# In the first mixer of a two-layer model, VectorE makes every lower weight part, and the closing scans of a head move behind the next head's gate projection

## The chip, the core and the metric

The kernel runs on one core of a Trainium2 chip. The metric is the device time of one execution in microseconds. Engine names in the rows: PE is TensorE, PEld its weight loads, DVE is VectorE, ACT is ScalarE, POOL is GpSimd, SP is SyncE, which issues the loads of weights.

## What is computed

A two-layer backbone over 256 latent tokens and 256 context tokens of width 1024. Layer 0 mixes tokens with a bidirectional gated linear recurrence, layer 1 with a spatial gate, and a mixture of 64 experts follows each mixer. The change touches the first mixer alone:

```python
def rglru_mixer(hx, hc, w_in, conv_w, conv_b, ..., w_out, ctx_out):
    gate_x, ux = jnp.split(hx @ w_in, 2, axis=-1)
    ux = dwconv_centred(ux, conv_w, conv_b)
    uc = dwconv_centred(hc @ w_in[:, RNN_WIDTH:], conv_w, conv_b)
    for d in range(2):                       # both directions
        a_c, b_c = lru_coeffs(flip(uc), ...)  # a = exp(log_a), b = sqrt(1 - a*a) * i * u
        h_c = linear_scan(a_c, b_c)          # h[t] = a[t] * h[t-1] + b[t]
        a_x, b_x = lru_coeffs(flip(ux), ...)
        b_x = b_x.at[:, 0].add(a_x[:, 0] * h_c[:, -1])
        yx = yx + flip(linear_scan(a_x, b_x))
    return (jax.nn.gelu(gate_x) * yx) @ w_out
```

The recurrence is 1280 wide, in five heads of 256.

## The kernel before

Instructions are issued in the order in which the program is written, each engine works its own list from the front, and an instruction that waits holds up all behind it on its engine.

**Products in three parts.** A product in full precision is three TensorE products of rounded parts: upper weight times upper input, upper weight times lower input, lower weight times upper input (`mm3`, L311 and on; all recorded at L307). The upper weight part `wh` is a rounding copy of a piece of 128x512 on ScalarE (L563). The lower part `wl` is the piece less `wh` (L564), on the engine that `eng` returns. `splitter` hands out pieces in order and makes each up to three ahead of its use; `wh` and `wl` have four buffers, so the fifth piece waits until TensorE has read the first. A tile of weights (1 MB) is four pieces.

**The stage.** After a start, in which the inputs are normalised and the first projection runs interleaved with small products for the modulation (`first_quarter`), `plan0` sets the order of five heads h = 0 to 4. For each: A(h) projects to the two halves (i = 0, 1) of the recurrence's input, C(h) projects to the gate, B(h) makes the recurrence's coefficients; one to four filler products (F, matrix tiles of the modulation, no lower parts) stand between them. Then four output tiles O(0) to O(3) use heads 0 to 3, and Q uses head 4.

- A(h) takes one tile. After each half, `conv` runs: ScalarE scales one tap (L753), VectorE adds three (L755, `uc`), casts the result to its upper part (L758, `us`) and subtracts for the lower part (L759).
- C(h) takes one tile and ends in a Gelu on ScalarE (L858).
- B(h) takes one tile and does two column blocks jt = 0, 1. For each, ScalarE computes tanh and exp from eight products (L817 to L823), then VectorE runs a **chain** of four operations of 128x1024 on `te`, `ta`, `ti` (L825 to L828). The block is put into `held`.
- `B_end` **closes** a block: a square root on ScalarE (L833), then on VectorE a product (L836), four scans of 128x256 (L840, L843) and a sum (L845). `release` closes the oldest held block. Before the change both blocks of head h-1 are closed at the end of A(h).
- `gated(h)` multiplies a closed head with its gate (L868, VectorE) and splits it into `zh` and `zl` (L869, L870): on GpSimd for heads 0 to 3, on VectorE for head 4.
- `decay`, issued once behind A(0), makes the recurrence's decay coefficients `nz` from `lam`: an exp on ScalarE (L789) and 27 VectorE operations of 128x20 (L790 to L802).

The chooser of the engine for `wl` before the change: the fillers have no lower parts, and all tiles of A, C, O and B go to GpSimd, those of Q to VectorE.

Of the kernel before, what the change touches and what calls it, by code (L numbers as in the profile page):

```python
# [14 lines left out]
AF = mybir.ActivationFunctionType  # L15
# [286 lines left out]
def _body(nc, tc, a, pp, rp, ps, ps1, dr):  # L302
    V, S, G, PE = nc.vector, nc.scalar, nc.gpsimd, nc.tensor
    st = Stream(nc)

    def mm(out, lhsT, rhs, start, stop):
        PE.matmul(out, lhsT, rhs, start=start, stop=stop, skip_group_check=True)  # L307

    def mm3(out, wh, wl, xh, xl, start, stop):

        mm(out, wh, xh, start, False)  # L311
        mm(out, wh, xl, False, False)
        mm(out, wl, xh, False, stop)

    def bank(shape=(P, 512)):
        return ps.tile(list(shape), F32, name="b")
# [22 lines left out]
    plan0, nf = [], 0  # L339
# [9 lines left out]
    for kind, i in plan0[1:]:  # L349
# [10 lines left out]
        elif kind == "F":  # L360
            l, c, k = fillers[i]
# [92 lines left out]
    def warm(func):  # L454

        S.activation(out=warm_t, in_=onesf[:, 0:1], func=func)
# [96 lines left out]
    def splitter(tmp, tiles, eng, bufs=4):  # L553

        out = []

        def get(q, last=None):
            while len(out) < min(q + 3, last or 4 * len(tiles)):
                i, c = divmod(len(out), 4)
                t = st.tile(tiles[i])[:, 512 * c:512 * c + 512]  # L560
                hi = tmp.tile([P, 512], F32R, name="wh", bufs=bufs)
                lo = tmp.tile([P, 512], F32R, name="wl", bufs=bufs)
                S.copy(out=hi, in_=t)  # L563
                eng(i, c).tensor_tensor(out=lo, in0=t, in1=hi.bitcast(F32), op=OP.subtract)  # L564
                out.append((hi, lo))
                if c == 3:
                    st.free(tiles[i])
            return out[max(q, 0)]

        return get  # L570

    def cut(parts, c):
        return [x[:, c * P:c * P + P] for x in parts]
# [63 lines left out]
    def mixer0(rx):  # L637
      with tc.tile_pool(name="m0", bufs=1) as mp, tc.tile_pool(name="m0t", bufs=2) as tp:
# [3 lines left out]
        def h0(x, k):  # L642
            return h0t[2 * x + k // 4][:, k % 4, :]
# [31 lines left out]
        for half in range(2):  # L675
            q = [qc[k // 4] if half else qx[:, k:k + 4] for k in (0, 4)]
# [3 lines left out]
            q = q[0]  # L680
# [20 lines left out]
        sx = mp.tile([P, 8], F32, name="sx")  # L701
        sc = mp.tile([P, 8], F32, name="sc")

        def split_eng(i, c):
            kind, j = plan0[users[i]]
            return G if kind in "ACOB" else V

        users = [i for i, e in enumerate(plan0) if e[0] != "F"]

        base = 8  # L710
        wq = splitter(tp, [2] + [base + i for i in users[1:]], split_eng)

        def first_quarter(b):

# [29 lines left out]
        def A(h, q):  # L744
            uc = tp.tile([P, 2, 2, T], F32, name="uc", bufs=2)
            us = tp.tile([P, 2, 2, 512], F32R, name="us", bufs=1)
            ucs[h] = uc, us

            def conv(i, p):
                ft = 2 * h + i  # L750
                pv = p.rearrange("p (s t) -> p s t", s=2)
                o = uc[:, i]
                S.activation(out=o, in_=pv, func=AF.Identity, scale=cw[:, 2, ft:ft + 1], bias=cb[:, ft:ft + 1])  # L753
                for kk, (d0, d1, s0_, s1_) in ((0, (2, T, 0, T - 2)), (1, (1, T, 0, T - 1)), (3, (0, T - 1, 1, T))):
                    V.scalar_tensor_tensor(out=o[:, :, d0:d1], in0=pv[:, :, s0_:s1_], scalar=cw[:, kk, ft:ft + 1],  # L755
                                           in1=o[:, :, d0:d1], op0=OP.mult, op1=OP.add)
                of = o.rearrange("p s t -> p (s t)")
                V.tensor_copy(out=us[:, 0, i, :], in_=of)  # L758
                V.tensor_tensor(out=us[:, 1, i, :], in0=of, in1=us[:, 0, i, :].bitcast(F32), op=OP.subtract)  # L759

            ps_ = [bank(), bank()]
            steps = [(i, k) for k in range(8) for i in range(2)] if h == 0 else [(i, k) for i in range(2) for k in range(8)]
            for i, k in steps:
                if h == 0 and i == 0 and k:
                    yield
                wc = divmod(2 * k + i if h == 0 else 8 * i + k, 4)
                mm3(ps_[i], *cut(wq(q + wc[0], 4 if h == 0 and k < 7 else None), wc[1]), h0(0, k), h0(1, k), k == 0, k == 7)
                if k == 7:
                    wq(q + 3 + 2 * i)
                    conv(i, ps_[i])  # L770
            release()
            release()

        held, done = deque(), []
        first_quarter(0)
        assert st.reserve("a_in") == 2
        a0 = A(0, 0)
# [26 lines left out]
        def B(h, q):  # L804
            warm(AF.Exp)
            uc, us = ucs.pop(h)
            y = ys[h] = tp.tile([P, 2, T], F32, name="hf", bufs=4)

            for jt in range(2):
                ft = 2 * h + jt  # L810
                ta, te, ti = (tp.tile([P, 2, 512], F32, name=n, bufs=2) for n in ("T", "Tt", "I"))
                for g in range(2):
                    for d in range(2):
                        p = bank()
                        for k in range(2):
                            mm3(p, *cut(wq(q + 2 * jt + g), 2 * d + k), us[:, 0, k, :], us[:, 1, k, :], k == 0, k == 1)
                        S.activation(out=(ta, ti)[g][:, d, :], in_=p, func=AF.Tanh, scale=0.5, bias=(rb_, ib_)[g][:, d, ft:ft + 1])  # L817
                if jt:
                    wq(q + 5)
                for d in range(2):  # L820
                    n1, n2 = nz[:, d, ft:ft + 1], nz2[:, d, ft:ft + 1]
                    S.activation(out=te[:, d, :], in_=ta[:, d, :], func=AF.Tanh, scale=n1, bias=n1)
                    S.activation(out=ta[:, d, :], in_=ta[:, d, :], func=AF.Exp, scale=n2, bias=n2)  # L823
                uv = uc[:, jt].rearrange("p s t -> p (s t)").unsqueeze(1).to_broadcast([P, 2, 512])
                V.scalar_tensor_tensor(out=te, in0=ta, scalar=1.0, in1=te, op0=OP.add, op1=OP.mult)  # L825
                V.tensor_scalar(out=ta, in0=te, scalar1=-1.0, scalar2=1.0, op0=OP.mult, op1=OP.add)
                V.scalar_tensor_tensor(out=te, in0=te, scalar=2.0, in1=te, op0=OP.subtract, op1=OP.mult)
                V.scalar_tensor_tensor(out=ti, in0=ti, scalar=1.0, in1=uv, op0=OP.add, op1=OP.mult)  # L828
                held.append((h, jt, y, ta, te, ti))

        def B_end(h, jt, y, ta, te, ti):

            S.activation(out=te, in_=te, func=AF.Sqrt, scale=-0.25)  # L833
            V.memset(te[:, 0, T:T + 1], 0.5)
            V.memset(te[:, 1, 2 * T - 1:2 * T], 0.5)
            V.tensor_tensor(out=ti, in0=ti, in1=te, op=OP.mult)  # L836
            for d in range(2):
                r_, s_, i_ = ta[:, d, :], te[:, d, :], ti[:, d, :]
                rv = (lambda z: z[:, ::-1]) if d else (lambda z: z)
                V.tensor_tensor_scan(rv(s_[:, T:]), rv(r_[:, T:]), rv(i_[:, T:]), 0.0, OP.mult, OP.add)  # L840
                last = T if d else 2 * T - 1
                dst = s_[:, :T] if d else y[:, jt, :]
                V.tensor_tensor_scan(rv(dst), rv(r_[:, :T]), rv(i_[:, :T]), s_[:, last:last + 1], OP.mult, OP.add)  # L843
                if d:
                    V.tensor_tensor(out=y[:, jt, :], in0=y[:, jt, :], in1=dst, op=OP.add)  # L845
            if jt:
                if h < 4:
                    done.append(h)
                else:
                    gated(h)  # L850

        def Cg(i, q):
            p = bank()
            for j in range(2):
                for k in range(8):
                    mm3(p[:, j * T:(j + 1) * T], *cut(wq(q + 2 * j + k // 4), k % 4), h0(0, k)[:, :T], h0(1, k)[:, :T], k == 0, k == 7)
            gs[i] = tp.tile([P, 2, T], F32, name="hf", bufs=4)
            S.activation(out=gs[i].rearrange("p f t -> p (f t)"), in_=p, func=AF.Gelu_apprx_tanh)  # L858

        ob = {}  # L860
        def release():
            if held:
                B_end(*held.popleft())

        def gated(h):
# [29 lines left out]
        for i, (kind, j) in enumerate(plan0):  # L895
            if kind == "F":
                l, c, k = fillers[j]
# [14 lines left out]
            n = st.reserve({"A": "a_in", "C": "a_in", "B": "gate", "O": "a_out", "Q": "a_out"}[kind])  # L912
# [688 lines left out]
    with tc.tile_pool(name="rx", bufs=1) as rx:  # L1601
        tail = mixer0(rx)
        tail = moe(0, tail)
        tail = mixer1(tail)
        moe(1, tail)
# [16 lines left out]
```

## Time and profile before

| | us |
|---|---|
| median of three runs (lowest to highest) | 1508.54 (1504.59 to 1512.67) |
| the profiled execution | 1504.02 |
| its span, first to last instruction | 1502.2 |
| PE busy in the span | 1410.3 (94%) |
| DVE busy | 766.5 (51%) |
| ACT busy | 518.9 (35%) |
| POOL busy | 433.7 (29%) |
| the first mixer, to its last update of x | 0 to 257.05 |

The shares are means over stages with different limits: the first mixer is the one stage in which VectorE and GpSimd are busy most of the time. What the change is worth is to be read in the first 257 us.

### The profile page before, as it was taken

To read this page: it belongs to the slowest core of one execution; us is meant where nothing else is said; L and a number is where in the kernel's file an instruction comes from. 1 tells how busy PE (TensorE), PEld (TensorE's weight loads), DVE (VectorE), ACT (ScalarE), POOL (GpSimd) and SP (SyncE) were. 2 spreads that over 40 slices of the span, in tenths; PEclk is the share of its full clock that TensorE was granted. 3 is DMA by queue.
4 is the path that set the end of the run, shared out by engine and by line. 5 is a ranking of instruction groups with operands and counts; after the bars stand their busy time and mean duration, and the time that the engine had idled before them with its cause. 6 is when DMAs were issued, how large, how long until landed. Compare 5 with 4: busy or idle time off the path is not lost.

```text
span 1502.2 us, 27457 instructions
## 1 busy us (share of the span) xinstructions
PE 1410.3 (94%) x10752; PEld 983.3 (65%) x10752; DVE 766.5 (51%) x1388; ACT 518.9 (35%) x901; POOL 433.7 (29%) x454
## 2 busy tenths in 40 slices
PE   5999898789999999999999999789999999999998
PEld 4767677546567565565747899666656666566665
DVE  6899997623343434334346686532425333333434
ACT  4767673321222222222225544422212212212232
POOL 1666665412222113221101361322212212211210
PEclk9999999899999999999999999899999999999998
DMA  9776575589998999999999854469998999999994
GB/s 376 280 278 228 224 308 224 231 318 377 381 418 358 421 420 406 421 394 420 420 418 380 320 169 153 140 231 391 362 396 358 421 421 409 406 402 422 420 420 168
DMA packets 77446, 514.88 MB, mean 343 GB/s; under 512 B 9856, under 2 KB 10240, under 8 KB 17024
## 3 DMA queue, kind: packets, MB, share of 16 engines
q1 hardware_dynamic: 74720, 508.91, 83.8%
q10 hardware_dynamic: 2592, 4.16, 0.8%
q8 instruction: 86, 1.41, 0.4%
q14 instruction: 48, 0.39, 0.1%
HBM read 511.99 MB, written 1.05 MB: 342 GB/s over the span
## 4 chain that ended last, share of the span: by engine, by line
PE 59%; issue 13%; POOL 3%; DVE 2%; DMA 2%; ACT 1%; ACTq 0%; POOLq 0%; SPq 0%; DVEq 0%
PE b L307 49%; PE s L307 10%; DMA wr<-in_m_gu 2%; POOL S L1399 1%; POOL wl L564 1%; PE b L1475 1%; DMA wr<-in_m_dn 1%; DVE wl L564 1%; DVE h L948 0%; ACT wh L563 0%; PE b L1587 0%; DVE v L1004 0%; DVE xT L1115 0%; DVE v L1067 0%; DVE u L956 0%
## 5 line engine op out<-in xcount | busy, mean ns | idle before, releaser
L564 POOL TENSOR_TENSOR wl<-wr,wh 128x512 fp32r<-128x512 f32 x134 | 208.2, 1570 | 537.0 <-ACT wh L563 534.8
L307 PE MATMUL b<-wr,xg 128*32 128x512 f32 (+2 forms) x1496 | 301.1, 602 | 8.2 <-DMA wr<-in_m_gu 6.3
L563 ACT CAST wh<-wr 128x512 fp32r<-128x512 f32 x256 | 152.4, 618 | 200.8 <-PE b L307 93.6
L307 PE MATMUL b<-wx,xg 128*32 128x512 f32 (+1 forms) x712 | 196.1, 599 | 0.0
L307 PEld LDWEIGHTS b<-wr,xg 128*32 128x32 f32 (+2 forms) x1496 | 83.3, 119 | 130.6 <-issue 107.2
L307 PE MATMUL s<-hh,wh 128*128 128x256 f32 x512 | 153.7, 300 | 6.4 <-ACT wh L563 6.4
L564 POOL TENSOR_TENSOR wl<-wx,wh 128x512 fp32r<-128x512 f32 x48 | 71.4, 1505 | 302.5 <-ACT wh L563 263.5
L1115 DVE SCALAR_TENSOR_TENSOR xT<-b,mod,xT 128x256 f32<-128x256 f32 x304 | 130.0, 478 | 49.1 <-PE b L307 43.2
L564 DVE TENSOR_TENSOR wl<-wr,wh 128x512 fp32r<-128x512 f32 x122 | 100.2, 838 | 104.3 <-ACT wh L563 104.2
L1491 DVE SCALAR_TENSOR_TENSOR Y<-b,gt,Y 128x512 fp32r<-128x512 f32 x88 | 66.1, 751 | 169.4 <-ACT Y L1490 169.4
L307 PE MATMUL s<-hh,wl 128*128 128x256 f32 x512 | 146.9, 287 | 3.4 <-POOL wl L564 3.4
L307 PE MATMUL b<-wr,ht 128*32 128x512 f32 (+2 forms) x752 | 148.1, 599 | 1.5 <-ACT ht L1477 1.4
L307 PE MATMUL s<-hl,wh 128*128 128x256 f32 x512 | 145.9, 285 | 0.0
L1468 DVE TENSOR_TENSOR h<-h,b 128x256 f32<-128x256 f32 x44 | 18.5, 420 | 205.3 <-ACT h L1467 205.3
L307 PEld LDWEIGHTS s<-hh,wh 128*128 128x128 f32 x512 | 99.4, 194 | 36.0 <-issue 28.3
L1490 ACT ACTIVATE Y<-b,gt 128x512 fp32r<-128x512 f32 x88 | 60.5, 687 | 136.0 <-PE b L307 136.0
L1467 ACT ACTIVATE h<-b 128x256 f32<-128x256 f32 x44 | 16.9, 383 | 256.4 <-PE b L307 256.4
L307 PEld LDWEIGHTS s<-hh,wl 128*128 128x128 f32 x512 | 99.4, 194 | 4.5 <-POOL wl L564 4.2
L307 PEld LDWEIGHTS s<-hl,wh 128*128 128x128 f32 x512 | 99.6, 194 | 0.4
L307 PE MATMUL b<-wx,ht 128*32 128x512 f32 (+2 forms) x352 | 99.1, 603 | 0.5 <-ACT ht L1477 0.5
L563 ACT CAST wh<-wx 128x512 fp32r<-128x512 f32 x112 | 66.5, 618 | 93.9 <-PE b L307 48.3
L1399 POOL TENSOR_SCALAR S<-cst,agq 128x32 fp32r<-128x32 f32 (+3 forms) x208 | 82.6, 421 | 49.4 <-PE b L307 49.3
(283 smaller groups left out, 2817.5 us busy)
## 6 DMA issues: line engine op xcount, KB each, us to landing
wr<-in_m_gu SPq DMA_DIRECT2D x173, 1024.0 KB, 11.6
wx<-in_m_gu SPq DMA_DIRECT2D x83, 1024.0 KB, 11.9
wr<-in_m_dn SPq DMA_DIRECT2D x82, 1024.0 KB, 10.8
wx<-in_m_dn SPq DMA_DIRECT2D x40, 1024.0 KB, 9.9
wr<-in_ada_w SPq DMA_DIRECT2D x31, 1024.0 KB, 7.8
wr<-in_a_in SPq DMA_DIRECT2D x10, 1024.0 KB, 8.7
wr<-in_ada SPq DMA_DIRECT2D x8, 1024.0 KB, 12.2
wr<-in_b_v SPq DMA_DIRECT2D x7, 1024.0 KB, 16.3
```

Of the source, the lines that this page charges most:

```text
L307: PE.matmul(out, lhsT, rhs, start=start, stop=stop, skip_group_check=True)
L563: S.copy(out=hi, in_=t)
L564: eng(i, c).tensor_tensor(out=lo, in0=t, in1=hi.bitcast(F32), op=OP.subtract)
L1115: V.scalar_tensor_tensor(out=xT[:, d, :], in0=y, scalar=mod[:, l, 5, d:d + 1], in1=xT[:, d, :], op0=OP.mult, op1=OP.add)
L1399: (G if b else V).tensor_scalar(out=s[:, tt, i * P + o:i * P + o + wd], in0=C["iota1"][:, j:j + wd], scalar1=agq[:, tt, q:q + 1], scalar2= ...
L1467: S.activation(out=h, in_=p[:, :256], func=AF.Silu)
L1468: V.tensor_tensor(out=h, in0=h, in1=p[:, 256:], op=OP.mult)
L1475: PE.transpose(p[:, k * P:(k + 1) * P], h[:, k * P:(k + 1) * P], ident)
L1490: S.activation(out=hi, in_=p, func=AF.Copy, scale=gts[g])
L1491: V.scalar_tensor_tensor(out=y[:, 1, 512 * c:512 * c + 512], in0=p, scalar=gts[g], in1=hi.bitcast(F32), op0=OP.mult, op1=OP.subtract)
```

## The change

1. All lower parts of the mixer's weights are made on VectorE (76 pieces move from GpSimd; the four of Q were there).
2. In `conv`, the cast to the upper part moves from VectorE to ScalarE (L758).
3. Pieces are split ahead: `ready(n)` makes all pieces up to the n-th, ahead of the convolutions, of the chains of B and of the closings.
4. A head's two closings move from the end of A(h) to the end of C(h), one ahead of one more split piece and one behind it. Their square roots (`roots`) stay at the end of A(h).

```diff
-        def split_eng(i, c):
-            kind, j = plan0[users[i]]
-            return G if kind in "ACOB" else V
-
         users = [i for i, e in enumerate(plan0) if e[0] != "F"]
 
         base = 8
-        wq = splitter(tp, [2] + [base + i for i in users[1:]], split_eng)
+        wq = splitter(tp, [2] + [base + i for i in users[1:]], lambda i, c: V)
+
+        def ready(n):
+
+            wq(n - 3)
...
                 of = o.rearrange("p s t -> p (s t)")
-                V.tensor_copy(out=us[:, 0, i, :], in_=of)
+                S.copy(out=us[:, 0, i, :], in_=of)
                 V.tensor_tensor(out=us[:, 1, i, :], in0=of, in1=us[:, 0, i, :].bitcast(F32), op=OP.subtract)
...
                 if k == 7:
-                    wq(q + 3 + 2 * i)
+                    ready(q + 6 + 2 * i)
                     conv(i, ps_[i])
-            release()
-            release()
+            roots()
...
-                if jt:
-                    wq(q + 5)
+
+                ready(q + 6 + 2 * jt)
                 for d in range(2):
...
+        def roots():
+
+            while len(rooted) < len(held):
+                te = held[len(rooted)][4]
+                S.activation(out=te, in_=te, func=AF.Sqrt, scale=-0.25)
+                rooted.append(te)
+
         def B_end(h, jt, y, ta, te, ti):
-
-            S.activation(out=te, in_=te, func=AF.Sqrt, scale=-0.25)
...
+            ready(q + 8)
             gs[i] = tp.tile([P, 2, T], F32, name="hf", bufs=4)
             S.activation(out=gs[i].rearrange("p f t -> p (f t)"), in_=p, func=AF.Gelu_apprx_tanh)
+            release()
+            ready(q + 9)
+            release()
 
         ob = {}
+
         def release():
             if held:
+                if not rooted:
+                    roots()
+                rooted.popleft()
                 B_end(*held.popleft())
```

TensorE's and SyncE's lists are the same before and after, but for which buffer a load goes to. Three places of the other lists matter.

**VectorE around the decay coefficients**, behind A(0): first before, then after. `s_...` and `lam` are the small 128x20 operands, `nz` the coefficients, `Tt` and `T` the operands of B(0)'s first chain, `wr_298` the weight tile of B(0) and `wr_382` that of A(1).

```order
L799 TENSOR_TENSOR s_185<-s_185,s_183 128x20
L800 TENSOR_SCALAR s_184<-lam 128x20
L801 SCALAR_TENSOR_TENSOR nz<-s_185,s_184 128x20
L802 TENSOR_SCALAR nz_182<-nz 128x20
L825 SCALAR_TENSOR_TENSOR Tt<-T,Tt 128x1024
```

```order
L798 TENSOR_TENSOR s_185<-s_185,s_183 128x20
L799 TENSOR_SCALAR s_184<-lam 128x20
L800 SCALAR_TENSOR_TENSOR nz<-s_185,s_184 128x20
L801 TENSOR_SCALAR nz_182<-nz 128x20
L564 TENSOR_TENSOR wl<-wr_298,wh 128x512 x4
L564 TENSOR_TENSOR wl<-wr_382,wh 128x512 x2
L824 SCALAR_TENSOR_TENSOR Tt<-T,Tt 128x1024
```

The four lower parts that B(0)'s products read, before on GpSimd's list, now stand on VectorE's list behind the last coefficient.

**ScalarE around A(2)'s second half and C(2)**, first before, then after. The weight tiles are C(2)'s (`wr_869` before, `wr_853` after) and B(2)'s (`wr_959`, `wr_963`); `hf<-b` is the Gelu, `Tt<-Tt` the square roots of head 1.

```order
L563 CAST wh<-wr_869 128x512 x2
L753 ACTIVATE uc<-b,cb,cw 128x512
L833 ACT_TABLE_LOAD
L833 ACTIVATE Tt<-Tt 128x1024 x2
L563 CAST wh<-wr_959 128x512 x2
L858 ACT_TABLE_LOAD
L858 ACTIVATE hf<-b 128x512
L563 CAST wh<-wr_959 128x512 x2
```

```order
L563 CAST wh<-wr_853 128x512 x2
L753 ACTIVATE uc<-b,cb,cw 128x512
L758 CAST us<-uc 128x512
L834 ACT_TABLE_LOAD
L834 ACTIVATE Tt<-Tt 128x1024 x2
L563 CAST wh<-wr_963 128x512 x4
L863 ACT_TABLE_LOAD
L863 ACTIVATE hf<-b 128x512
```

The cast of `uc`, which reads what VectorE adds, now stands ahead of the table load, the square roots and the upper parts of B(2).

**VectorE from A(2)'s convolutions to the closings of head 1**, first before, then after; `wr_853` is C(2)'s tile, `wr_963` B(2)'s, and the MEMSET opens a closing.

```order
L755 SCALAR_TENSOR_TENSOR uc<-b,cw,uc 128x2x254
L755 SCALAR_TENSOR_TENSOR uc<-b,cw,uc 128x2x255 x2
L758 CAST us<-uc 128x512
L759 TENSOR_TENSOR us<-uc,us 128x512
L834 MEMSET Tt 128x1
```

```order
L564 TENSOR_TENSOR wl<-wr_853,wh 128x512 x2
L755 SCALAR_TENSOR_TENSOR uc<-b,cw,uc 128x2x254
L755 SCALAR_TENSOR_TENSOR uc<-b,cw,uc 128x2x255 x2
L759 TENSOR_TENSOR us<-uc,us 128x512
L564 TENSOR_TENSOR wl<-wr_963,wh 128x512 x4
L838 MEMSET Tt 128x1
```

The pieces show the second half of A(2). Between the convolution and the first closing VectorE now has the four lower parts of B(2), whose upper parts ScalarE makes behind its square roots.

## Rows read from the trace of the kernel before

**Rows 1.** Windows: us, busy us of PE, PEld, DVE, ACT, POOL; PEclk, DMA share, GB/s.

```profile
0.00:61.53 61.53, 45.56 (x436) 35.72 (x440) 44.46 (x117) 34.36 (x56) 17.14 (x16) 1.00 0.96 381
61.53:95.92 34.39, 33.40 (x191) 24.48 (x184) 33.44 (x35) 25.53 (x38) 22.43 (x12) 1.00 0.64 254
95.92:134.21 38.29, 34.90 (x181) 25.63 (x180) 35.19 (x38) 25.57 (x38) 25.72 (x15) 0.91 0.68 252
...
170.78:208.37 37.59, 32.84 (x166) 25.22 (x163) 35.63 (x37) 24.30 (x36) 25.15 (x14) 0.91 0.56 224
208.37:257.05 48.68, 43.23 (x322) 37.28 (x320) 42.13 (x45) 23.12 (x39) 36.63 (x23) 0.96 0.65 259
```

**Rows 2.** Waits, 20 to 257 us: total us, times, longest.

```profile
PE b L307 <- POOL wl L564: 13.2, 9, 4.7
```

**Rows 3.** Timeline, PE, 97.5 to 102: start, us, work, idle before.

```profile
101.54 0.79 PE L307 MATMUL b<-wx,wl 128*128 128x512 f32 x1 [3.39 <-POOL wl L564]
```

**Rows 4.** Windows: the stretch of lowered clock behind that wait.

```profile
100.38:107.20 6.82, 5.66 (x13) 4.46 (x14) 5.99 (x4) 3.46 (x5) 6.82 (x4) 0.50 0.08 32
```

**Rows 5.** Timeline, DVE, head 2's chain to head 2's closing.

```profile
134.21 1.22 DVE L825 SCALAR_TENSOR_TENSOR Tt<-T,Tt 128x1024 f32<-128x1024 f32 x1 [0.74 <-ACT T L823]
135.47 1.66 DVE L826 TENSOR_SCALAR T<-Tt 128x1024 f32<-128x1024 f32 x1
137.16 2.18 DVE L827 SCALAR_TENSOR_TENSOR Tt<-Tt 128x1024 f32<-128x1024 f32 x1
...
152.24 0.43 DVE L758 CAST us<-uc 128x512 fp32r<-128x512 f32 x1
152.70 0.69 DVE L759 TENSOR_TENSOR us<-uc,us 128x512 fp32r<-128x512 f32 x1
153.31 2.31 DVE L755 SCALAR_TENSOR_TENSOR uc<-b,cw,uc 128x508 f32<-128x508 f32 x3
...
164.35 0.06 DVE L835 MEMSET Tt<- 128x1 f32 x1
...
168.94 0.22 DVE L919 CAST identb<-cst 128x128 bf16<-128x128 f32 x1
```

**Rows 6.** Timeline, POOL, the same head.

```profile
136.54 15.84 POOL L564 TENSOR_TENSOR wl<-wr,wh 128x512 fp32r<-128x512 f32 x8
```

**Rows 7.** Timeline, DVE, Q's lower parts, with GpSimd at rest.

```profile
245.79 2.49 DVE L564 TENSOR_TENSOR wl<-wx,wh 128x512 fp32r<-128x512 f32 x4
```

**Rows 8.** Timeline, ACT, behind A(3)'s second half.

```profile
150.50 1.28 ACT L833 ACT_TABLE_LOAD   x1
151.79 2.01 ACT L833 ACTIVATE Tt<-Tt 128x1024 f32<-128x1024 f32 x2
153.71 1.12 ACT L563 CAST wh<-wr 128x512 fp32r<-128x512 f32 x2
```

**Rows 9.** Timeline, DVE, the coefficients and the first chain.

```profile
50.85 0.17 DVE L790 TENSOR_SCALAR s<-s 128x20 f32<-128x20 f32 x1
...
54.49 1.26 DVE L797 TENSOR_TENSOR s<-s,s 128x20 f32<-128x20 f32 x1
...
58.22 0.18 DVE L802 TENSOR_SCALAR nz<-nz 128x20 f32<-128x20 f32 x1
61.53 1.23 DVE L825 SCALAR_TENSOR_TENSOR Tt<-T,Tt 128x1024 f32<-128x1024 f32 x1 [3.14 <-ACT T L823]
```

**Rows 10.** Timeline, PE, B(0): first and last of 32 merged rows, 48 products.

```profile
49.78 0.63 PE L307 MATMUL b<-us,wh 128*128 128x512 f32 x2
...
60.91 0.39 PE L307 MATMUL b<-us,wl 128*128 128x512 f32 x1
```

**Rows 11.** Timeline, PE, one step of Q (12 products, 8 router products).

```profile
252.15 0.36 PE L307 MATMUL b<-zh,wh 128*128 128x256 f32 x1
...
253.66 1.00 PE L307 MATMUL s<-rws,xT 128*128 128x64 f32 x8
254.47 0.37 PE L307 MATMUL b<-zh,wh 128*128 128x256 f32 x1
```

More of the change, by code (lines that the diff above doesn't have):

```diff
@@ L768, in A @@
                 if k == 7:
-                    wq(q + 3 + 2 * i)
+                    ready(q + 6 + 2 * i)
                     conv(i, ps_[i])
-            release()
-            release()
-        held, done = deque(), []
+            roots()
+        held, rooted, done = deque(), deque(), []
         first_quarter(0)
```

## The prediction

> **What bounds the kernel now.** I cut the start of the span into windows at the first operation of each head's chain on VectorE (61.53 for head 0, 208.37 for head 4). The reader is to see that from 61.53 to 208.37 VectorE is busy nearly all the time (33.4 of 34.4 us, 35.2 of 38.3, 35.6 of 37.6), while TensorE has more room [rows 1]. So VectorE sets the pace of the heads. TensorE's own idle time in the mixer stands in the list of waits: 13.2 us, in nine waits, for lower parts from GpSimd [rows 2]. One is 3.39 us at 101.54 [rows 3], and around it the granted clock fell to 0.50, the lower of the two levels (1.2 of 2.4 GHz), for 6.82 us [rows 4], which costs TensorE up to 3.4 us more. Behind the mixer TensorE's and SyncE's lists are unchanged, and the expert loads wait for the router's result, so I let the rest of the span shift as it is: what counts is when the mixer's last update of x ends, 257.05 before.
>
> The timeline of VectorE shows why it is full. With GpSimd making lower parts (eight in 15.84 us [rows 6]), an operation of 128x1024 takes 2.18 us; beside no subtraction of GpSimd's it takes 1.22 [rows 5]. The lower part itself, on VectorE with GpSimd at rest, takes 2.49/4 = 0.62 [rows 7]. So GpSimd's parts cost VectorE about as much in collisions as making them would. The Trainium skill ("SBUF — State Buffer", section "Who interferes with whom") says that a VectorE instruction with two SBUF inputs contends with a GpSimd instruction that reads SBUF, and that whichever issues second is blocked until the first is through. The collided rows agree; it speaks for the change, and is the root of the first rival.
>
> **Change, part by part: the heads.** VectorE's work for one head after the change, from free rows:
> - two closings, 164.35 to 168.94 = 4.6 each [rows 5]: 9.2;
> - twelve lower parts (A, C, B) at 0.62 [rows 7]: 7.4;
> - two chains of four. The first operation is 1.22 free. The second, a one-input operation, was not seen free: it lies between the 0.43 of a cast of half its width and its collided 1.66 [rows 5]; I take 0.75, near the cast, since it is the same kind of work. The other two read like the first, 1.2. That is 4.4 a chain. GpSimd keeps the split of the closed head (`zh`, `zl`), which falls on the first chain: one collision, 2.18 - 1.22 = 1.0. Together 9.8;
> - two convolutions, 2.34 for three taps and 0.61 for the subtraction (152.70 to 153.31) [rows 5]: 5.9; their casts, 0.46 each, leave;
> - gating product and modulation's transposes, an estimate by the 0.69 of an operation of like width: 1.35.
>
> Sum 33.65. The period before is (208.37 - 61.53)/4 = 36.7 [rows 1]. If that were all, a head would gain 3 us. But the new order makes VectorE wait twice for ScalarE. After three taps of the first half it waits for ScalarE's cast (0.60 and two handovers, 0.75). After the second half ScalarE does, one behind the other: that cast (0.6), the table load (1.28), two square roots (151.79 to 153.71 = 1.92), and the upper part of B's first piece (0.6) [rows 8]; only then can VectorE make the lower part, and all closings stand behind these lower parts. With handovers 4.55, of which the subtraction covers 0.6: 3.95 idle. Before, ScalarE ran table load and roots beside VectorE's work, with no such wait. A head then takes 33.65 + 0.75 + 3.95 = 38.35, 1.65 more than before, four times: **+6.6**. What is queued behind: VectorE's closings, so B's tanh, which needs the closed block's buffers, and TensorE, which needs B's first lower part and idles some 2.7 us there. Bounds: with the second operation of the chain at 0.43 and half of the long wait covered 35.8, with it at 1.3 and a handover more 39.5: -3.6 to +11.
>
> On the table load the Trainium skill ("ScalarE: Activation LUTs", section "What ACT_TABLE_LOAD costs") gives 1283 ns and a drain of some 1380 ns behind it. The trace agrees on the load, 1.28, but the root starts 0.01 us behind it [rows 8], so I put nothing for the drain; by the page each head would be another 1.4 longer, 5.5 in four.
>
> **The start.** Before, GpSimd made B(0)'s lower parts while VectorE worked through the decay coefficients, and B(0)'s products ran from 49.78 to 61.30 [rows 10]. The first chain waited until 61.53 for tanh and exp, which themselves waited for the coefficients (done at 58.40) [rows 9]. Now B(0)'s lower parts stand behind the last coefficient. When is that done? Eight lower parts more ahead of it 5.0; two casts fewer -0.9; two waits for ScalarE's casts 1.5; the exp of `decay` now stands behind the second cast, 1.0 by a load and two short operations against the subtraction beside it; the first lower part waits for its upper part behind ScalarE's first inputs, of which idle time elsewhere takes a part back, 0.8 by estimate; six operations that last 0.7 to 1.1 longer than their twins go free, such as 1.26 against the 0.18 of a like one [rows 9], -5.6. That is +1.8: 60.2. First lower part 0.7: 60.9. Half of B(0)'s 48 products, 5.6 less the 0.45 that need no lower part: 66.1. Last tanh, one upper part, and four tanh and exp (58.40 to 61.53 = 3.1 [rows 9]): 4.3, so the first chain starts at 70.4 instead of 61.53: **+8.9**. Bounds 7.5 and 12: the sum of small terms is good to 1.5, and TensorE, idle for some 8 us ahead of B(0), may run at the lower clock.
>
> **The end.** From head 4's first chain the mixer took 48.68 [rows 1]. After: chain 5.4 with its collision, two lower parts 1.25, second chain 4.4, transpose and router weights 1.8 (estimate), closing 4.6, and only now O(1)'s first lower part, 0.7: 18.1. TensorE is through with O(0) near 9 and idles 9 us. Twelve products take 1.5 [rows 11], a tile of output 6. Two of O(2)'s pieces wait for buffers, that is for O(1)'s second piece and an upper part: 22.4. Then the second closing 4.6, product, cast and subtraction 1.7, O(2)'s third piece 0.7: 29.4. Half of O(2) and O(3), 9: 38.4. Q's four steps of 2.32 [rows 11], the first without router products, and the last update: 48.1. So **-0.6**: VectorE free of collisions gives back here what its lower parts cost. Bounds -4 and +2.
>
> **Clock.** Three stretches like [rows 4] are in the time before. The gaps ahead of B(0) and O(1) are longer than the 3.39 that led to one, so I count a half of 2.5 for each: **+2.5**, bounds 0 and 6. In the heads VectorE is late and TensorE has room.
>
> **Sum**: 8.9 + 6.6 - 0.6 + 2.5 = 17.4, against the profiled execution's 1504.0: 1521.4. Its time is 4.5 under the median of the runs shown, 1508.5, which scatter by 4 to either side; I carry a part of that and forecast 1523, 1.0% slower.
>
> **Rivals.**
> 1. *Not slower: freedom from collisions is all that counts.* Place: the closings and chains of heads 0 to 3. If ScalarE's casts and roots come in time, a head takes the 33.65 of VectorE's work: 4 x -3.05 = -12.2, with the start 8.9 and the end -0.6: 1500. For: VectorE is 92 to 97% busy and collided rows are near twice the free ones [rows 1, 5]. Against: ScalarE's list is in order, and its roots stand behind a cast that reads VectorE's last tap. It decides once a head takes under 34.6. The page on SBUF named above would give this sign.
> 2. *No change.* The long wait is half covered, a head takes 36.2: -2 + 8.9 - 0.6 = 1510. For: VectorE could run late enough that ScalarE's list is ahead. Against: the cast needs VectorE's own last tap, so lateness of VectorE doesn't cover it.
> 3. *Slower still: the clock is on the path.* Each head's gap of 2.7 lowers the clock, and B's slower products delay tanh and so the chain by 2 a head; with 3.4 at B(0) and 2.9 at O(1): 8.9 + 6.6 - 0.6 + 8 + 6.3 = 29, 1533. For: the 3.39 gap did it [rows 3, 4]. Against: tanh has to wait for the closing anyway.
>
> **Chances.** Mine 0.63, rival 1 0.14 (half of that with something more from the end, and so faster), rival 2 0.08, rival 3 0.15. About 0.5% (7.5 us) is what a measurement of this kernel tells from no change. Slower: mine and rival 3, 0.78. Same 0.15. Faster 0.07. Of all, 1509 to 1536 leaves out rival 1 and a little at either end; the likeliest case's own range, from the bounds of its terms, is 1512 to 1534.
>
> **What would show it.** In the profile after: no lower parts on GpSimd in the mixer and chain operations of 1.2; the first chain near 70 and a TensorE gap of some 8 us ahead of B(0), put down to VectorE's `wl`; VectorE idle for near 4 us in each head ahead of B's first `wl`, put down to ScalarE's `wh`, behind the roots; periods of 38; a TensorE gap near 9 us between O(0) and O(1). Wrong, if the periods are 34 to 35, or if the first chain starts near 62.

## The result, and the profile after

The changed kernel takes 1522.82 us in the median (1518.38 to 1528.61), the kernel before, run beside it, 1508.1 (1502.97 to 1512.67): a ratio of 1.0106, 95% interval 1.0083 to 1.0129. It is slower by 1.1%, against the forecast of 1523.

The windows of the profiled execution after, cut as [rows 1] at the first chain operation of each head (same columns):

```profile
0.00:73.45 73.45, 47.98 (x432) 37.63 (x432) 46.77 (x129) 36.12 (x60) 0.19 (x4) 0.95 0.81 319
73.45:110.81 37.36, 36.76 (x208) 26.00 (x207) 31.15 (x45) 26.16 (x40) 0.55 (x1) 1.00 0.67 256
110.81:149.29 38.48, 34.19 (x180) 24.71 (x178) 33.08 (x47) 27.12 (x41) 3.06 (x3) 0.96 0.62 236
149.29:188.07 38.78, 36.15 (x191) 26.31 (x188) 33.48 (x51) 27.42 (x42) 3.17 (x3) 0.96 0.57 218
188.07:225.73 37.66, 33.77 (x190) 24.19 (x192) 32.36 (x46) 25.15 (x38) 3.17 (x3) 1.00 0.56 219
225.73:274.15 48.42, 37.77 (x299) 35.95 (x291) 37.28 (x59) 21.28 (x36) 6.35 (x7) 0.89 0.69 264
```

Against [rows 1] the start is 73.45 - 61.53 = 11.9 us longer, the four heads together (225.73 - 73.45) - 146.84 = 5.4 longer, the end 0.3 shorter. The mixer ends at 274.15, 17.1 later; the rest of the span is 1.5 shorter, and the span grows by 15.6. VectorE is no longer busy all the time in a head (32.36 of 37.66 us), and GpSimd has almost left (3 us a head for 25). Over the whole span its busy time fell from 433.7 to 298.6, VectorE's a little, and the kernel is slower all the same; the page's busy times (share of the span):

```profile
PE 1413.5 (93%) x10752; PEld 987.7 (65%) x10752; DVE 754.0 (50%) x1454; ACT 522.7 (34%) x911; POOL 298.6 (20%) x378
```

The waits of TensorE from 40 to 275 us (total, times, longest): GpSimd's nine of [rows 2] are gone, and more stand in their place, for VectorE and for ScalarE.

```profile
PE b L307 <- DVE wl L564: 16.1, 8, 5.9
PE b L307 <- ACT wh L563: 13.8, 6, 2.8
```

The timeline of VectorE at the start and in head 2, and of ScalarE there:

```profile
60.60 0.18 DVE L801 TENSOR_SCALAR nz<-nz 128x20 f32<-128x20 f32 x1
60.71 2.50 DVE L564 TENSOR_TENSOR wl<-wr,wh 128x512 fp32r<-128x512 f32 x4
...
73.45 1.23 DVE L824 SCALAR_TENSOR_TENSOR Tt<-T,Tt 128x1024 f32<-128x1024 f32 x1 [2.43 <-ACT T L822]
...
131.80 0.69 DVE L759 TENSOR_TENSOR us<-uc,us 128x512 fp32r<-128x512 f32 x1 [0.74 <-ACT us L758]
135.62 2.50 DVE L564 TENSOR_TENSOR wl<-wr,wh 128x512 fp32r<-128x512 f32 x4 [3.13 <-ACT wh L563]
138.07 0.06 DVE L838 MEMSET Tt<- 128x1 f32 x1
```

```profile
131.15 0.62 ACT L758 CAST us<-uc 128x512 fp32r<-128x512 f32 x1 [2.52 <-DVE uc L755]
131.79 1.28 ACT L834 ACT_TABLE_LOAD   x1
133.08 2.00 ACT L834 ACTIVATE Tt<-Tt 128x1024 f32<-128x1024 f32 x2
134.99 1.12 ACT L563 CAST wh<-wr 128x512 fp32r<-128x512 f32 x2
```

Read the two together: ScalarE's cast of `us` waits for VectorE's last tap, then table load, roots and B's upper part run behind it one after the other, and VectorE stands for 3.13 us until the first upper part is there. Heads 0 to 3 each show it, with two waits of 0.74 for the cast itself.

TensorE ahead of B(0), and ahead of O(1); then the stretch of lowered clock that begins in the first of these gaps (columns as in [rows 4]):

```profile
55.82 0.73 PE L307 MATMUL b<-us,wh 128*128 128x512 f32 x2 [2.82 <-ACT wh L563]
61.46 0.79 PE L307 MATMUL b<-us,wl 128*128 128x512 f32 x1 [4.91 <-DVE wl L564]
...
237.42 0.39 PE L307 MATMUL b<-zh,wh 128*128 128x256 f32 x1 [2.45 <-ACT wh L563]
243.81 0.58 PE L307 MATMUL b<-zh,wl 128*128 128x256 f32 x1 [5.89 <-DVE wl L564]
```

```profile
57.90:64.70 6.80, 3.24 (x8) 2.57 (x9) 4.86 (x19) 1.33 (x2) 0.00 (x0) 0.50 0.10 23
```

### The profile page after: what moved, and what is told of

Read it like the earlier page. It is cut to its first block, busy times and chain, and to the rows that moved or that the text cites. A ratio compares the mean times of both kernels' runs of the same rounds, so it can differ in the third digit from the quotient of the medians.

```text
span 1517.8 us, 27439 instructions
## 1 busy us (share of the span) xinstructions
PE 1413.5 (93%) x10752; PEld 987.7 (65%) x10752; DVE 754.0 (50%) x1454; ACT 522.7 (34%) x911; POOL 298.6 (20%) x378
## 4 chain that ended last, share of the span: by engine, by line
PE 60%; issue 12%; DVE 2%; POOL 2%; DMA 2%; ACT 1%; ACTq 0%; SPq 0%; POOLq 0%; DVEq 0%
PE b L307 49%; PE s L307 10%; DMA wr<-in_m_gu 2%; POOL S L1411 1%; POOL wl L564 1%; PE b L1487 1%; DVE wl L564 1%; DVE h L960 0%; ACT wh L563 0%; PE b L1599 0%; DVE v L1016 0%; DVE xT L1127 0%; DVE v L1079 0%; DVE u L968 0%; ACT h L1078 0%
## 5 line engine op out<-in xcount | busy, mean ns | idle before, releaser
L307 PE MATMUL b<-wr,xg 128*32 128x512 f32 (+2 forms) x1512 | 307.7, 602 | 6.8 <-DMA wr<-in_m_gu 5.7
L564 DVE TENSOR_TENSOR wl<-wr,wh 128x512 fp32r<-128x512 f32 x191 | 149.0, 806 | 127.4 <-ACT wh L563 127.3
L307 PE MATMUL b<-wx,xg 128*32 128x512 f32 (+2 forms) x696 | 200.6, 600 | 0.7 <-ACT xg L1427 0.7
L564 POOL TENSOR_TENSOR wl<-wr,wh 128x512 fp32r<-128x512 f32 x69 | 94.1, 1374 | 489.2 <-ACT wh L563 487.6
L307 PE MATMUL b<-wr,ht 128*32 128x512 f32 (+2 forms) x728 | 153.6, 595 | 1.4 <-ACT ht L1489 1.4
L1503 DVE SCALAR_TENSOR_TENSOR Y<-b,gt,Y 128x512 fp32r<-128x512 f32 x88 | 66.1, 751 | 166.4 <-ACT Y L1502 166.4
L564 POOL TENSOR_TENSOR wl<-wx,wh 128x512 fp32r<-128x512 f32 x37 | 49.9, 1358 | 281.8 <-ACT wh L563 242.8
L1479 ACT ACTIVATE h<-b 128x256 f32<-128x256 f32 x44 | 16.9, 383 | 255.8 <-PE b L307 255.8
L563 ACT CAST wh<-wx 128x512 fp32r<-128x512 f32 x108 | 64.8, 620 | 103.4 <-PE b L307 50.9
L307 PE MATMUL b<-S,xt 128*128 128x256 f32 x704 | 94.1, 287 | 0.0
```

Of the source, the lines that this page charges most:

```text
L1479: S.activation(out=h, in_=p[:, :256], func=AF.Silu)
L1503: V.scalar_tensor_tensor(out=y[:, 1, 512 * c:512 * c + 512], in0=p, scalar=gts[g], in1=hi.bitcast(F32), op0=OP.mult, op1=OP.subtract)
```

## The experiments

All ratios are to the kernel before, run on the same chip. My theory was the one on record: the start (lower parts behind the coefficients), the heads (ScalarE's cast ahead of roots and upper parts), and a little at the end. The rival was that VectorE, which makes 76 more pieces, is itself the bound.

### One part of the change undone

**The cast back on VectorE (e2).**

```diff
-                S.copy(out=us[:, 0, i, :], in_=of)
+                V.tensor_copy(out=us[:, 0, i, :], in_=of)
```

> The changed kernel, with the upper part of the convolved input cast on VectorE again, as before the change. Theory (ScalarE's list, in which table load and roots stand behind a cast that reads VectorE's last tap, makes VectorE idle 3.1 us and 2 times 0.74 us a head): VectorE pays 0.9 a head for two casts and saves most of 4.6, so the period falls from 38.1 to 34.6 to 35.5, four times 2.6 to 3.5, and the start gains 1 to 1.5: 12 us less, 1509 to 1512. Rival (the closings behind the gate projection make VectorE wait for TensorE, whatever the cast): the period stays over 37 and under 4 us come back.

Measured: 1507.37 us, ratio 1.0018 (1.0003 to 1.0032). The windows of its heads 0 to 3:

```profile
71.73:107.47 35.74, 35.74 (x204) 25.48 (x203) 32.00 (x47) 25.67 (x38) 2.30 (x2) 1.00 0.69 257
107.47:141.97 34.50, 33.63 (x187) 24.88 (x186) 32.66 (x49) 26.27 (x39) 0.45 (x1) 1.00 0.71 274
141.97:177.06 35.09, 34.21 (x189) 25.27 (x188) 34.26 (x53) 26.68 (x40) 3.18 (x3) 1.00 0.61 241
177.06:211.03 33.97, 31.78 (x178) 23.32 (x181) 33.15 (x48) 23.70 (x35) 3.18 (x3) 1.00 0.63 242
```

The mean period is (211.03 - 71.73)/4 = 34.8 for 38.1, though VectorE does more. Two casts of 0.43 on VectorE cost less than what they made it wait on ScalarE. Undoing this one line takes back 0.0088 of the 0.0106 that the whole change costs.

**A closing at the end of O(0) and of O(2) (e3)**, in place of one at the start of O(0) and one at the end of O(1).

```diff
-            if i == 0:
-                release()
...
-            if i == 1:
+            if i in (0, 2):
                 release()
```

> The changed kernel, with head 4's two closings issued at the ends of O(0) and O(2) instead of at the start of O(0) and the end of O(1), so that VectorE makes the next output tile's lower parts ahead of each. Theory (TensorE idles 8 us behind O(0) because those parts stand behind a closing): the gap shrinks to 4 to 5 us, Q starts 2 to 3 us earlier: 2 to 5 us less with the clock, 1518 to 1521. Rival (Q's start hangs on the closings, which VectorE reaches no earlier): no change within 1.5 us.

Measured: 1517.91 us, ratio 1.0090 (1.0071 to 1.0108); from head 4's first chain to the mixer's end 46.3 us instead of 48.42. TensorE's waits ahead of O(1) are now

```profile
239.26 0.58 PE L307 MATMUL b<-zh,wl 128*128 128x256 f32 x1 [3.04 <-DVE wl L564]
245.10 0.39 PE L307 MATMUL b<-zh,wl 128*128 128x256 f32 x1 [1.30 <-DVE wl L564]
```

in place of 2.45 and 5.89: what O(1) waits for is a lower part behind a closing. It is worth 2 us. A third wait, ahead of O(2)'s third piece, stays (2.56 us, 2.31 in the changed kernel).

**The coefficients behind B(0)'s first pieces (e1)**: `decay` is called inside C(0), behind its `ready`.

```diff
             ready(q + 8)
+            if i == 0:
+                decay()
...
-                decay()
```

> The changed kernel, with the decay coefficients issued inside C(0), behind B(0)'s four pieces, instead of ahead of C(0). Theory (the order of VectorE's list makes the start late): B(0)'s first lower part is ready near 55 instead of 60.7, its products no longer wait for the coefficients, and the first chain, now held by the coefficients and ScalarE, starts near 67.5 instead of 73.45: 6 us less, 1516 to 1518. Rival (the lowered clock from 57.9 to 64.7 made the start late, and the gap only shows it): TensorE idles ahead of B(0) anyway, and less than 2 us come back.

Measured: 1516.66 us, ratio 1.0082 (1.0064 to 1.0100). The first chain comes at 67.65, 5.8 earlier, but the first period is 39.48 instead of 37.36, so 3.9 are left at the mixer's end. The rival, that the lowered clock made the start late and the gap only shows it, falls: TensorE's gap ahead of B(0) shrinks to 1.00 us, and the granted clock is 1.00 from 60 to 68 us. What takes 2.1 us back in the first period is seen in the timeline of ScalarE in head 1, its DMA issues (ACTq) among it:

```profile
95.70 0.62 ACT L563 CAST wh<-wr 128x512 fp32r<-128x512 f32 x1 [0.96 <-PE b L307]
95.71 0.33 ACTq L447 DMA_DIRECT2D cst<-in_cst  x1
...
99.02 0.62 ACTq L930 DMA_DIRECT2D rw<-in_r_w  x1
99.67 1.28 ACT L456 ACT_TABLE_LOAD   x1 [3.35 <-issue]
```

Five small loads that the program issues from ScalarE in head 1 stand ahead of B(1)'s table load and tanh, and VectorE's next chain then waits 2.13 for the exp. They are tried below.

**All three together (e4)**, against the question whether their gains add up.

> The three edits together. Theory: they mend different stretches and add up, 6 + 12 + 3 = 21 us less than the changed kernel, 1500 to 1504, which is 4 to 8 us faster than the kernel before. Rival (the stretches share one path, so that what one saves is lost to the next): the sum comes to under 14 us, and the kernel is no faster than before the change.

Measured: 1498.63 us, ratio 0.9959 (0.9941 to 0.9976); first chain 65.67, mean period 35.06, end part 46.23. By the ratios the single gains are 0.0088, 0.0016 and 0.0024, in sum 0.0128; together 0.0147 came: they add up, and the 0.0019 more is within what the measurements scatter. The first chain, 65.67, is still 4.1 later than before; which of the lower parts ahead of it make these 4.1 us, no run here splits.

### One part done alone in the kernel before

**All lower parts on VectorE and nothing else (f1)**: `split_eng` returns `V`.

```diff
-            return G if kind in "ACOB" else V
+            return V
```

> The kernel before, with one edit: all lower parts on VectorE, in the old order of the program. Theory (not the engine but the place in VectorE's list decides): collisions go and chain operations fall to 1.2, but B's lower parts stand behind both closings, so that TensorE waits some 9 us for them in each head, and behind the coefficients at the start. The period is 41 to 43, the start 9 to 12 later: 25 to 38 us slower than the kernel before, 1533 to 1546. Rival (VectorE sets the pace and freedom from collisions is what counts): periods of 35, within 5 us of the kernel before or faster.

Measured: 1537.57 us, ratio 1.0198 (1.0153 to 1.0242), mean period 42.5. The waits from 60 to 240 us, and one chain's first row:

```profile
PEld b L307 <- DVE wl L564: 35.2, 9, 6.5
ACT T L817 <- PE b L307: 34.6, 10, 6.6
DVE Tt L825 <- ACT T L823: 31.8, 8, 9.0
```

```profile
112.47 1.23 DVE L825 SCALAR_TENSOR_TENSOR Tt<-T,Tt 128x1024 f32<-128x1024 f32 x1 [8.14 <-ACT T L823]
```

The operation lasts 1.23, free of collisions, and that is no help. Read the waits as one ring: B's lower parts now stand behind the closings on VectorE, TensorE waits for them, ScalarE's tanh for TensorE, VectorE's chain for tanh. The splitting ahead and the moved closings are there to mend this. By the ratios they do: with them, and the cast left on VectorE, 1.0198 becomes 1.0018.

**The cast on ScalarE and nothing else (f2).**

```diff
-                V.tensor_copy(out=us[:, 0, i, :], in_=of)
+                S.copy(out=us[:, 0, i, :], in_=of)
```

> The kernel before, with one edit: the cast to the upper part of the convolved input on ScalarE. Theory: VectorE waits 0.75 for each cast and 1.6 for the first root, which now stands behind the second cast, and saves two casts that took 0.5 to 1.4: 1 to 2 us a head more, 3 to 9 us slower, 1511 to 1517. Rival (VectorE is the bound, and every operation that leaves it is a gain): 3 to 4 us faster.

Measured: 1520.18 us, ratio 1.0083 (1.0053 to 1.0113): more than I expected. The periods grow by 3.1 to 39.8, and the first chain comes 3.6 later. VectorE's timeline in head 2:

```profile
123.65 0.69 DVE L759 TENSOR_TENSOR us<-uc,us 128x512 fp32r<-128x512 f32 x1 [0.74 <-ACT us L758]
125.36 2.31 DVE L755 SCALAR_TENSOR_TENSOR uc<-b,cw,uc 128x508 f32<-128x508 f32 x3 [1.02 <-ACT uc L753]
128.42 0.69 DVE L759 TENSOR_TENSOR us<-uc,us 128x512 fp32r<-128x512 f32 x1 [0.74 <-ACT us L758]
130.82 0.06 DVE L834 MEMSET Tt<- 128x1 f32 x1 [1.71 <-ACT Tt L833]
```

I had reckoned with the two waits of 0.74. The other two are the same cast again: ScalarE, held until the last tap, comes later to what stands behind it, the second half's own tap (1.02) and the roots (1.71). So the cast costs 0.8 to 0.9% in either kernel, and the new order of closings is not needed for it.

### The start

After e1 the 11.9 us of the start, 3 more than my 8.9, were still to be settled. In the trace after, a cast of A(1)'s piece on ScalarE waits until 65.35 for a buffer, and B(0)'s table load and tanh stand behind it; I took this for half of the miss. The test leaves that piece to B(0).

```diff
-            ready(q + 9)
+            if i:
+                ready(q + 9)
```

> The changed kernel, but C(0) does not ask for A(1)'s first piece (ready(q + 9) is left out for i == 0), so that ScalarE's table load and first tanh of B(0) stand ahead of that cast instead of behind it. My reading of the changed kernel: the cast waits until 65.35 us for B(0)'s first piece to be read, and the load of 1.28 us and the warm of 0.20 us run behind it, so tanh starts at 67.39 though its sum is ready near 65.4. Then here: the load ends near 60.5, tanh starts at 65.3 to 66.0, the first chain comes at 71.4 to 72.1 instead of 73.45, and the kernel takes 1520.5 to 1522 us (ratio 1.009 to 1.010). Rival: what the start took over my forecast is TensorE's lower clock alone, then tanh waits for TensorE anyway and the first chain stays within 0.5 us of 73.45, ratio 1.0106.

Measured: 1523.04 us, ratio 1.0108 (1.0085 to 1.0130), first chain 73.21. My reading fell. ScalarE's timeline:

```profile
59.28 1.28 ACT L456 ACT_TABLE_LOAD   x1
...
...
68.34 0.69 ACT L816 ACTIVATE I<-b,ib__111 128x512 f32<-128x512 f32 x1 [0.67 <-PE b L307]
68.92 1.13 ACT L563 CAST wh<-wr 128x512 fp32r<-128x512 f32 x2
```

With the load out of the way tanh simply waits for TensorE, the last until 68.34, and the cast left out comes back behind it. TensorE, idle until 61.48 and at a granted clock of 0.50 from 58.0 to 64.8, as in the changed kernel, is what sets the first chain; how much of it is the gap and how much the clock, this run does not split.

**B(0)'s lower parts alone on GpSimd (e6)**, the changed kernel otherwise:

```diff
-        wq = splitter(tp, [2] + [base + i for i in users[1:]], lambda i, c: V)
+        b0 = users.index(plan0.index(("B", 0)))
+        wq = splitter(tp, [2] + [base + i for i in users[1:]], lambda i, c: G if i == b0 else V)
```

> The changed kernel, but the four lower parts of B(0)'s first tile alone are made on GpSimd, beside VectorE's decay coefficients instead of behind them. Theory (the start is the lower parts behind the coefficients): TensorE begins B(0) near 57 to 58 instead of 61.46, and the first chain is then set by the coefficients, which collide with GpSimd's parts three or four times (about 1 us each) and end near 63 to 64.5: first chain 66 to 68 instead of 73.45, later chains unchanged in period, 1515.5 to 1518 us (ratio 1.006 to 1.0075). Rival: the collisions take back what the parts gave, or the late cast of A(1)'s piece sets the tanh anyway: first chain above 71, ratio over 1.0095.

Measured: 1518.04 us, ratio 1.0085 (1.0067 to 1.0102), first chain 69.41: 4 us earlier, 1.4 later than expected. Coefficients that take 0.18 free collide again:

```profile
59.18 1.20 DVE L798 TENSOR_SCALAR s<-s 128x20 f32<-128x20 f32 x1
60.41 1.20 DVE L797 TENSOR_TENSOR s<-s,s 128x20 f32<-128x20 f32 x1
61.65 0.17 DVE L798 TENSOR_SCALAR s<-s 128x20 f32<-128x20 f32 x1
```

Four such rows, 1.0 longer each, and a start 0.7 later put the last coefficient at 65.53, where the changed kernel has 60.78; ScalarE's tanh of the block are through at 65.75, so both hold the chain. Still, TensorE's gap for a lower part shrinks to 0.64 us. So the place of B(0)'s lower parts is the largest single part of the start's loss: 5.8 of the 11.9 us by e1. With the cast and the closings of O as in e2 and e3, this made (g1)

> The changed kernel with the cast of the convolution's upper part back on VectorE, one closing at the end of O(0) and one at the end of O(2), and B(0)'s first tile split on GpSimd with the coefficients in their place. Additive theory: first chain 64.5 to 66.5, periods near 34.9, the piece of 2 us that the moved coefficients lost in the first period is not lost here, tail 46.3: 1495 to 1499 us, ratio 0.993 to 0.996, the same as or up to 3 us under the version with the three edits. Rival: the collisions on the coefficients keep the first chain at 67.5 or later: 1499 to 1502.

Measured: 1500.51 us, ratio 0.9961 (0.9946 to 0.9976), a little above what I expected: the first chain is as forecast, 66.13, but the first period is 36.4, so the loss there is not the moved coefficients'. It is the small loads again, 2.56 us on ScalarE ahead of B(1)'s table load.

### The five small loads

They go to GpSimd, which now has little to do, in the version with the moved coefficients (e7) and in the one with all three edits (g2); all five issues change alike.

```diff
-        S.dma_start(cst[:, P:], a["cst"][:, P:])
+        G.dma_start(cst[:, P:], a["cst"][:, P:])
```

> The version with the coefficients moved behind the first piece of B(0), but the five small loads of head 1 (constants, gains, router bias and weights) are issued by GpSimd instead of ScalarE. Theory (in that version ScalarE stood 3.35 us at these issues, behind a cast, ahead of B(1)'s tanh, and that took back 2.1 us in the first period): first period 37.3 to 37.7 instead of 39.48, the other periods and the tail as in the changed kernel, 1514 to 1516 us, ratio 1.005 to 1.007. Rival: B(1)'s tanh waits there for the products or for the cast of A(2)'s piece in any case: first period stays near 39.4 and the ratio at 1.008. Second rival: GpSimd has nothing ahead of these loads and issues them while the weight loads fill the DMA engines, so the first chain comes up to 1 us later than 67.65 and takes half of the gain.

> The version with all three edits (1498.6 us), and the five small loads of head 1 issued by GpSimd instead of ScalarE. Theory: first period 34.5 to 35.2 instead of 36.69, the rest unchanged: 1496 to 1497.5 us, ratio 0.994 to 0.995. Rival: B(1)'s tanh waits for the cast of A(2)'s piece, which waits for TensorE, in any case: period 36.5 and 1498.5 us.

Measured: 1519.15 us, ratio 1.0077 (1.0053 to 1.0101), and 1496.08 us, ratio 0.9918 (0.9901 to 0.9935). The first periods fall as forecast, 39.48 to 37.27 and 36.68 to 33.93. But the first chains come at 70.58 and 67.54, 2.9 and 1.9 later, more than I allowed: GpSimd, with nothing ahead, issues the loads from 1.27 us, among the program's first. They are 0.73 MB in all, and the input of the context, loaded at the same time, now lands 9.7 us behind its issue in g2 where it took 6.9 in e4. So in the first pair nothing is gained. The last run puts the loads one head later, behind the split of head 0's output on GpSimd:

```diff
-                if j == 1:
+                if j == 2:
                     late_small()
```

> The last version (all three edits, small loads on GpSimd) with the five small loads written one head later, so that on GpSimd's list they stand behind the split of head 0's gated output and not at the program's start. Theory: they are issued near 100 us, the start is again that of the version with the three edits (first chain 65.5 to 66.2 instead of 67.54), the first period stays at 33.9 to 34.5: 1493.5 to 1495.5 us, ratio 0.990 to 0.9925. Rival: what the loads cost the start was not their place but chance in the weights' arrival, then the first chain stays near 67.5 and the time at 1496; or ScalarE's freed place in head 1 is what GpSimd's issues beside VectorE take back, then the second or third period rises by 0.5 or more.

Measured: 1494.55 us, ratio 0.9919 (0.9892 to 0.9945). GpSimd's first of these issues in g2, then here:

```profile
1.27 0.75 POOL L447 DMA_DIRECT2D cst<-in_cst  x1 [0.82 <-POOLq L1624]
...
101.90 0.75 POOL L447 DMA_DIRECT2D cst<-in_cst  x1
```

The context lands after 6.8 us again. The start and the first two periods:

```profile
0.00:65.60 65.60, 47.88 (x436) 36.92 (x440) 47.44 (x132) 35.18 (x58) 0.19 (x4) 0.97 0.91 358
65.60:99.16 33.56, 33.56 (x192) 24.70 (x184) 31.84 (x48) 25.56 (x38) 0.45 (x1) 1.00 0.65 254
99.16:134.03 34.87, 34.87 (x197) 25.32 (x196) 33.94 (x51) 26.36 (x39) 5.99 (x8) 1.00 0.79 289
```

Both gains are there, the early start and the short first period, and GpSimd's issues cost VectorE at most 0.4 in the second. Against g2 the whole gains nothing by the ratios (0.9919 for 0.9918; the 1.5 us between the two times are within what the measurements scatter), since g2's end part was 1.5 shorter (44.75 for 46.22); why, I did not settle. These last two versions beat the kernel before by 0.8% and the changed kernel by 1.9%.

## Why the prediction was right

The mechanism and its places were right. That the time came out within 0.2 us of the forecast is luck: with what the lowered clock cost taken out of start and end (below), the terms were off by +1.4 (start), -1.2 (heads), -2.1 (end) and +1.5 (clock), which cancel to 17.1 us for 17.4 in the mixer, and the rest of the span, which I had let stand, is 1.5 shorter.

- **Heads**, forecast +6.6, measured +5.4. Right in mechanism and place. I forecast waits of 0.75 and 3.95 a head, the second with the cast of the second half in it; the rows show 0.74, and then 0.74 and 3.13 on either side of the subtraction, 3.87. From the end of the last tap, 131.07, to the first lower part, 135.62, it is 4.55, as forecast. What is left of a head, 38.07 - 4.61 = 33.5, was forecast at 33.65. So waits and work came out 0.1 and 0.2 under in a head, which makes the 1.2 in four. With the cast put back (e2), 3.2 a head come back. I put the waits down to the new order; f2 shows that the cast makes as large a loss in the old one.
- **Start**, forecast +8.9, measured +11.9, within its bounds (to 12); this term was mis-sized. By its steps: coefficients done at 60.8 for 60.2; first lower part read from 61.46; half of B(0)'s products through at 68.3 instead of 66.1, of which the lowered clock makes 1.6 (6.8 us for 5.2); the last tanh to the chain 5.1 for 4.3. I had counted 1.25 for the clock under its own heading, so 1.8 of the start is missed. That ScalarE's table load would explain it fell with e5.
- **End**, forecast -0.6, measured -0.3. O(1)'s first lower part was forecast 18.1 behind head 4's chain: 243.81 - 225.73 = 18.1. The gap of 9 us shows as 2.45 and 5.89, with two products between. Behind it two misses cancel: O(2)'s third piece is read at 257.24, 31.5 behind the chain instead of 29.4, and from there to the end it takes 16.9 instead of 18.7.
- **Clock**, forecast +2.5. Length times what the granted clock lacks of 1, summed over the windows, is 12.1 us after (3.7, 1.5, 1.6, 5.3) and 8.8 before (3.4, 3.4 and 1.9 [rows 1]). The start's part costs 1.6. In the end O(1)'s first 23 products take 5.1 us at a granted clock of 0.50 (243.81 to 248.89), where 23 of O(0)'s take 2.7 at 1.00 (229.23 to 231.95): 2.4 more, and the second closing waits for them (it opens 24.3 behind the chain instead of 22.4). So the two gaps cost 4.0, not 2.5, inside the start and the end.
- **Rival 1** (freedom from collisions is all that counts, 1500, decided at a period of 34.6) needed ScalarE's casts to come in time, and they did not. Its mechanism is real: chain operations after are 1.22 to 1.23 where GpSimd is at rest, and with the cast back on VectorE, at 34.8, the kernel stands 0.2% over before; with the other edits it wins. The Trainium skill ("SBUF — State Buffer", section "Who interferes with whom") has VectorE's two-input operations contend with a GpSimd instruction that reads SBUF, and scalar operations that run in a two-port mode with GpSimd too. The rows agree: beside GpSimd's split of `zh` and `zl`, a two-input operation takes 1.63 for 1.22 and a scalar one 1.65 for 0.69, as here in head 4 of the changed kernel; in which mode the scalar one ran, no row says.

```profile
225.73 1.63 DVE L824 SCALAR_TENSOR_TENSOR Tt<-T,Tt 128x1024 f32<-128x1024 f32 x1
227.40 1.65 DVE L825 TENSOR_SCALAR T<-Tt 128x1024 f32<-128x1024 f32 x1
...
232.56 1.22 DVE L824 SCALAR_TENSOR_TENSOR Tt<-T,Tt 128x1024 f32<-128x1024 f32 x1
233.81 0.69 DVE L825 TENSOR_SCALAR T<-Tt 128x1024 f32<-128x1024 f32 x1
```

- **Rival 2** (the long wait half covered) fell: nothing of it is covered. (Its own sum, with half of 3.95 taken off, gives a head of 36.4 and 1511, not 36.2 and 1510.) **Rival 3** (clock on the path of the heads) fell: TensorE's waits of 2.6 are there in heads 1 to 3 (0.60 in head 0) and the clock is at 0.96 in heads 1 and 2, but no period is over the forecast 38.35 by more than 0.5.
- The drain that the Trainium skill ("ScalarE: Activation LUTs", section "What ACT_TABLE_LOAD costs") counts with a table load would add 1.4 to each long wait. The trace shows it on neither side of the load: the cast ahead ends at 131.77, the load runs from 131.79 for 1.28, the root starts at 133.08.

## What to carry to other kernels

An operation moved to an engine with time to spare still joins that engine's list. Here a cast of 0.43 us, moved from the busiest engine to one that is idle for some 30% of a head, cost 3 us a head, since it waits for the engine that it came from and everything behind it (table load, roots, next upper part) waits too. Ask of each moved instruction when its input is ready and what stands behind it until then, and when a stall is mended look one step on for whoever is late next: here five small loads, which held up no chain until VectorE came earlier, and were in the way of the first inputs once they sat on an empty queue.

## What I had not expected of the hardware

A free scalar operation of 128x1024 on VectorE takes 0.69 us, little over half of the 1.22 of a two-input one, and a collision costs it as much as the other or more (1.66 beside 2.18 [rows 5], 1.65 beside 1.63 in head 4 above). In proportion tiny ones lose most: 128x20 takes 0.18 free and 1.20 beside GpSimd's lower part, about as long as that part itself (four in 5.01). And five small loads issued by GpSimd from 1.27 us, 0.5 to 0.75 us of issue each, put the first chain 2 to 3 us back; issued at 101.9 and later, they cost at most 0.4.
